# Rows of softmax maxima written into the query operand by one masked VectorE instruction instead of a copy and a transfer

## The chip, the cores and the metric

One core of a Trainium2 chip runs the whole program. The metric is device time in microseconds (us) of one execution, the median over repeated runs. Engines are named as in the profile: PE is TensorE, PEld its weight loads, DVE is VectorE, ACT is ScalarE, POOL is GpSimd, SP is SyncE, which only issues transfers here. All transfers of ACT's and SP's queues share 16 DMA engines.

## The reference, cut to what matters

Two decoder layers over 2048 tokens of width 1024. Layer 0 mixes tokens by multi-head latent attention (12 heads, 64 + 32 rotary key columns), layer 1 by forgetting attention (12 heads of 64, with a cumulative log forget gate added to the logits). Each layer also has 4 heads of cross-attention into 256 memory tokens. All are softmax attentions:

```python
s = einsum('bqhd,bkhd->bhqk', q_i, k) * scale          # + F[t] - F[s] in layer 1
s = where(key_pos <= q_pos, s, -inf)                   # not for memory heads
p = softmax(s, axis=-1)
out = einsum('bhqk,bkhd->bqhd', p, v)
```

Then the heads are gated by silu(gate), projected, normalised and added to the residual stream. The softmax needs, for each query, some number close to its maximal logit that is subtracted before the exponential.

## The kernel before, in words

Layer 0 runs `proj_a` (input projection), `up_a` (up-projection of the latents to q, k and v), `attention`, `out_proj`; layer 1 runs `proj_b`, `attention`, `out_proj`. Float32 operands are split into a high and a low part (`hi` L195, `lo` L214), so that products of rounded parts add up to nearly full precision (`mm3` L247 issues three products for one). Outside the attention the tile framework orders the instructions of every engine by its own estimate of times; inside `run_units` the order is the one in which the code is written (L1151, `manual_schedule`).

An attention is cut into units (`Unit`, L1470): one head and 512 queries, 4 units a causal head and 4 a memory head, 64 units a layer. A unit goes through these steps.

- `q_dma` (L1483): SP loads the queries into an operand of the unit (head dimensions on partitions, 512 queries in the free dimension). Operands are a ring of a few tiles.
- `max_closures` (L1517): for each 128 queries, score products (L1560, for memory heads L1537) of 512 keys at a time go to PSUM, and DVE reduces each to its maximum (L1526). `nm` (L1569) joins several chunks (L1571). The result is a tile `nm` of 128 queries by 4 columns, negated.
- `nm_row` (L1573): one product with the identity (L1576) turns the 128x4 tile into 4 rows of 128 in PSUM, DVE copies them to a small tile `nr` (L1578), and ACT's queue issues a transfer of 2 KB (L1579) that lays the four rows one after the other into a single partition of the query operand, `nmrow`, right behind the head dimensions (partition 64 or 96). The key operand has a row of ones there (`k_ones` L1034, in layer 1 the first of the rows `fr` that `forget` stores at L986), so that the logit product itself subtracts the maximum.
- the logits: `s_logits` (L1677) with two or three products a block (`passes`, L1686), keys on PSUM partitions and queries in the free dimension; ACT's exponential reads PSUM (L1628, in the early units L1668), ACT copies to f16 (L198), POOL or DVE takes the remainder (L220).
- the values: `pv_steps` (L1689, products at L1702), `finish` (L1706) with the division and, every second head, a store by SP.

In layer 1 the key operand holds 9 rows behind the 64 head dimensions: the ones and 8 forget rows. `attention` (L1061) builds in each query tile `qb` the matching rows `ind`, one for the two forget rows of the unit's block and zero elsewhere; the row of maxima is written over the first of them. The maxima themselves use a copy of the operand in which that row stays zero.

Some memory units run before the attention proper, from `att_start` (L1002) through `run_early` (L1236), among the last projection products: 8 in layer 0, 12 in layer 1 (`MEM_EARLY`, L50). There the query loads are issued two units ahead and the rows of maxima one unit ahead. The others stand in the attention's list behind certain units (`MEM_AFTER`, L52); `MEM_FIRST` (L51) would put some at its front and is 0.

`run_units` (L1269) walks through the logit steps of all units in order and puts between them the score products of later units, up to `AHEAD` = 5 units ahead, as many columns as the ratio of score to logit columns and a lead demand. The `nm_row` of a unit is put in after 1024 more score columns (`ROW_AFTER`, L1281), and at the latest before the unit's own logits (L1376). On each engine the instructions are then executed in that order: what stands behind a waiting instruction waits too.

Names in the profile: `bA`, `bR`, `bQ`, `bG`, `bS` are views of the large slots of the on-chip memory (queries, keys, probabilities and `nr` alike), `banks` is PSUM, `idr` the identity, `nm` and `mx` the maxima, `frd` the forget rows, `qbs`, `qs`, `qms`, `vsp`, `ws` tensors in device memory.

Of the kernel before, what the change touches and what calls it, by code (L numbers as in the profile page):

```python
# [39 lines left out]
MEMW = 256  # L40
MEMH = 4
VC = 2 * DH + 1
EPS = 1e-6
THETA = 10000.0
LEAD = {0: 5.0, 1: 5.0}
# [1 line left out]
AHEAD = 5  # L47
MORE_Q = 6
PV_AHEAD = 120
MEM_EARLY = {0: 8, 1: 12}  # L50
MEM_FIRST = {0: 0, 1: 0}  # L51
MEM_AFTER = {0: (2, 3), 1: (1, 3)}  # L52
POOL_SHARE = {"mla": 0.45, "fox": 0.75, "mem": 0.5}
RUNUP = 1.7
ROW_AFTER = 1024
VALUES_AFTER = 3 * 1024
LOGP = 8.0 * math.log(2.0)
NEG = -1.0e30
# [130 lines left out]
class Trunk:  # L189
# [64 lines left out]
    def constants(self, ctx):  # L254
        tc, nc = self.tc, self.nc
        cp = self.cp = ctx.enter_context(tc.tile_pool(name="consts", bufs=1))
        self.pool = ctx.enter_context(tc.tile_pool(name="slots", bufs=1))
        self.psum = ctx.enter_context(tc.tile_pool(name="banks", bufs=1, space=PSUM)).tile([P, 8 * G], F32, name="banks")
        self.sm = ctx.enter_context(tc.tile_pool(name="small", bufs=3))
        idf = cp.tile([P, P], F32, name="idf")  # L260
        nc.gpsimd.memset(idf, 0.0)
        nc.gpsimd.affine_select(out=idf, in_=idf, compare_op=ALU.not_equal, fill=1.0, base=0,
                                pattern=[[-1, P]], channel_multiplier=1)
        idr = cp.tile([P, P], F32R, name="idr")
        nc.vector.tensor_copy(idr, idf)
        idb = cp.tile([P, P], BF16, name="idb")
        nc.vector.tensor_copy(idb, idf)
        mkq = cp.tile([P, P], BF16, name="mkq")
        nc.gpsimd.memset(mkq, 0.0)
        nc.gpsimd.affine_select(out=mkq, in_=mkq, compare_op=ALU.is_ge, fill=NEG, base=0,  # L270
                                pattern=[[1, P]], channel_multiplier=-1)
        self.mqk = cp.tile([P, P], BF16, name="mqk")
        nc.gpsimd.memset(self.mqk, 0.0)
        nc.gpsimd.affine_select(out=self.mqk, in_=self.mqk, compare_op=ALU.is_ge, fill=NEG, base=0,
                                pattern=[[-1, P]], channel_multiplier=1)
        ones = cp.tile([P, P], F32, name="ones")
        nc.gpsimd.memset(ones, 1.0)
        self.vmax = [cp.tile([P, 1], F32, name=f"vmax{l}") for l in range(4)]
        self.vscale = [cp.tile([P, 2], F32, name=f"vsc{l}") for l in range(4)]
        for t in self.vmax:  # L280
            nc.vector.memset(t, 0.0)
        nc.scalar.activation(cp.tile([P, 1], F32, name="one"), ones[:, 0:1], AF.Sqrt)
        self.idf, self.idr, self.idb, self.mkq, self.ones = idf, idr, idb, mkq, ones
        dp = ctx.enter_context(tc.tile_pool(name="scratch", bufs=1, space=DRAM))
        self.cs = dp.tile([P, 5, 2, S], F32, name="cs")
        self.qs = [dp.tile([P, 2, S], F32, name=f"qs{c}") for c in range(6)]
        self.ks = [dp.tile([P, 2, S], F32, name=f"ks{c}") for c in range(6)]
        self.qrs = dp.tile([HEADS, 2, HR, 2, S], F32, name="qrs")
        self.krs = dp.tile([ROPE, 2, S], F32, name="krs")
        self.qbs = [dp.tile([P, 2, S], F32, name=f"qbs{c}") for c in range(6)]  # L290
        self.kbs = [dp.tile([P, 2, S], F32, name=f"kbs{c}") for c in range(6)]
        self.fr = dp.tile([HEADS, 1 + 2 * NG, S], F32R, name="frd")
        self.vs = [dp.tile([S, HEADS * DH], F32, name=f"vs{l}") for l in range(2)]
        self.vsp = dp.tile([HEADS, P, NT, VC + 1], F16, name="vsp")
        self.qms = [[dp.tile([P, 2, S], F32, name=f"qms{l}_{c}") for c in range(2)] for l in range(2)]
        self.gs = [dp.tile([S, D], F32, name=f"gs{l}") for l in range(2)]
        self.kms = [dp.tile([DH, 2, MEMH, NMEM], F32, name=f"kms{l}") for l in range(2)]
        self.vms = [dp.tile([NMEM, MEMW], F32, name=f"vms{l}") for l in range(2)]
        self.ys = [dp.tile([S, D], F32, name=f"ys{l}") for l in range(2)]
        self.ws = dp.tile([KC, 2, P, D], F32, name="ws")  # L300
        self.h1 = [dp.tile([P, D], F32, name=f"h1_{t}") for t in range(NT)]
        self.cos, self.sin = (cp.tile([P, NT, HR], F32, name=x) for x in ("cos", "sin"))
        self.gq = cp.tile([P, 5], F32, name="gq")
        self.ssq = cp.tile([P, 2, NT], F32, name="ssq")
        self.rtok = cp.tile([P, 2, NT], F32, name="rtok")
# [645 lines left out]
    def forget(self, tp, tb, fpp, fl):  # L951
# [31 lines left out]
        nc.vector.tensor_copy(one, self.ones[0:HEADS, 0:1].to_broadcast([HEADS, G]))  # L983
        for b in range(NG):
            sl = slice(b * G, (b + 1) * G)
            nc.gpsimd.dma_start(out=self.fr[:, 0, sl], in_=one)  # L986
            for g in range(NG):
                d = tb.tile([HEADS, G], F32, name="fd", tag="fd")
                nc.vector.tensor_scalar(d, F[:, sl], F[:, g * G:g * G + 1], -math.sqrt(DH), op0=ALU.subtract, op1=ALU.mult)
                dh = tb.tile([HEADS, G], F32R, name="fdh", tag="fdh")  # L990
                nc.vector.tensor_copy(dh, d)
                dl = tb.tile([HEADS, G], F32R, name="fdl", tag="fdl")
                self.lo("dve", dl, d, dh)
                nc.gpsimd.dma_start(out=self.fr[:, 1 + 2 * g, sl], in_=dh)
                nc.gpsimd.dma_start(out=self.fr[:, 2 + 2 * g, sl], in_=dl)

    def load_r(self, dst, src):

# [3 lines left out]
    def att_start(self, l):  # L1002
# [14 lines left out]
        ap["qq"] = Turn(*(Later(lambda b=b, k=k: b.tile([P, 2, G], F32R, name=f"qq{k}")) for k, b in enumerate(qqs)))  # L1017
        ap["ymp"], ap["sp"] = ymp, sp
        ap["ym"] = Turn(*(ymp.tile([P, 4, 2 * DH], F32, name=f"ym{k}") for k in range(4)))
        ap["nr"] = Turn(*(nrp.tile([4, P], F32R, name=f"nr{k}") for k in range(4)))  # L1020
        ap["vrm"] = Turn(vrp.tile([P, MEMH * NMEM // P, DH], F32, name="vrm"))
        ap["pm"], ap["ps"], ap["pv"] = self.banks(2, 3), self.banks(5, 6), self.banks(0)
        self.l, self.yt = l, {}
# [8 lines left out]

    def k_ones(self, j):
        k = self.k_t[j]  # L1034
        row = k[DH:DH + 1, 1] if j == "m" else k[QK:QK + 1, 0] if self.l == 0 else None
        if row is not None:
            for b in range(0, row.shape[-1], G):
                self.hi("pool", row[:, b:b + G], self.ones[0:1, 0:1].to_broadcast([1, G]))

    def v_ones(self, j):  # L1040
        self.nc.gpsimd.memset(self.v_t[j][:, :, 2 * DH:VC + 1], 1.0)
# [18 lines left out]

    def attention(self):  # L1061
        nc, l, ap, B = self.nc, self.l, self.ap, self.box
        nb = DH + 1 + 2 * NG
        v0, yb = self.v0, B("A6" if l == 0 else "R0")
        ap["y"] = Turn(*(yb.tile([P, 4, 2 * DH], F32, name=f"y{k}") for k in range(4)))
        self.kv_place("1", B("A3" if l == 0 else "A6", r=True), yb if l == 0 else B("Q"))
# [7 lines left out]
        if l:  # L1074
# [2 lines left out]
            qb = B("A3", r=True), B("A0", r=True)  # L1077
            self.qb_t = [qb[j // NG].tile([nb, 2, G], F32R, name=f"qb{j}") for j in range(2 * NG)]
            for g in range(NG):
                ind = v0.tile([1 + 2 * NG, G], F32, name="ind")  # L1080
                nc.gpsimd.memset(ind, 1.0)
                for lo_b, hi_b in ((-(1 + 2 * g), 0), (0, 2 + 2 * g)):
                    nc.gpsimd.affine_select(out=ind, in_=ind, compare_op=ALU.is_ge, fill=0.0, base=lo_b + hi_b,
                                            pattern=[[0, G]], channel_multiplier=1 if lo_b else -1)
                for j in (g, g + NG):
# [150 lines left out]
def run_early(mem, objs):  # L1236
# [11 lines left out]
    def ends(m):  # L1248
        while len(pend) > m:
            o, s, box, _ = pend.pop(0)  # L1250
            with K.tc.high_priority(offset=PV_AHEAD):
                o.pv_steps([(s, box)])
            o.finish()
    for u in objs[:2]:
        u.q_dma()
    rows(objs[0])
    for k, u in enumerate(objs):
        if k + 2 < len(objs):
            objs[k + 2].q_dma()
        if k + 1 < len(objs):  # L1260
            rows(objs[k + 1])
        for pre, f, _ in u.main_closures():
            pre()
            f(pend)
# [133 lines left out]
class Head:  # L1398
# [7 lines left out]
    def prep(self):  # L1406
# [29 lines left out]

        def k_const():
            if kind == "fox":
                K.load_r(kt[DH:DH + 1 + 2 * NG, 1], K.fr[h].bitcast(F32))

        def v_load(a, b):
            nc.sync.dma_start(out=vt[:, a:b], in_=K.vsp[h, :, a:b])
# [27 lines left out]
class Unit:  # L1470
# [12 lines left out]
    def q_dma(self):  # L1483
# [5 lines left out]
        if self.kind == "fox":  # L1489
            src = K.qbs[h // 2][r, :, sl]  # L1490
            qa = self.q.get()
            qb = K.qb_t[g + NG * (h % 2)]
            nb = DH + 1 + 2 * NG
            K.load_r(qb[0:DH], src)
            K.load_r(qa, src[:, 0].unsqueeze(0).to_broadcast([2, DH, G]))
            self.mx_ops = ((qb[:, 0], nb), (kb, nb))
            self.nmrow = qb[DH:DH + 1, 1]
            self.passes = [((ka, P), (qa, P)), ((kb, nb), (qb[:, 1], nb))]
            return
        qq = self.q.get()  # L1500
# [1 line left out]
        if self.kind == "mla":  # L1502
            K.load_r(qq[0:NOPE], K.qs[h // 2][r, :, sl])
            K.load_r(qq[NOPE:QK], K.qrs[h, :, :, :, sl])
            self.nmrow = qh[QK:QK + 1]
            self.passes = [((ka, QK + 1), (qh, QK + 1)), ((kb, QK), (qh, QK)), ((ka, QK), (ql, QK))]
            self.mx_ops = ((qh, QK), (ka, QK))
        else:
            src = K.qms[l][h // 2][r, :, sl]
            K.load_r(qq[0:DH], src)  # L1510
            K.load_r(qh[DH:P], src[:, 0])
            self.nmrow = ql[DH:DH + 1]
            self.passes = [((ka, P), (qh, P)), ((kb, DH + 1), (ql, DH + 1))]
            self.mx_ops = ((qh, DH), (kb, DH))


    def max_closures(self):  # L1517
# [2 lines left out]
        out = []  # L1520

        def start():
            self.nmv = K.sm.tile([P, 4], F32R, name="nm", tag="nm", bufs=AHEAD + 2)

        def reduce(to, ps, negate):
            nc.vector.tensor_reduce(out=to, in_=ps, axis=AX.X, op=ALU.max, negate=negate)  # L1526
# [45 lines left out]

    def nm_row(self):  # L1573
        K, nc = self.K, self.K.nc
        ps = K.ap["pm"].tile([4, P], F32, name="pn", tag="pm")
        nc.tensor.matmul(ps, lhsT=self.nmv, rhs=K.idr, start=True, stop=True)  # L1576
        nr = K.ap["nr"].next()
        nc.vector.tensor_copy(nr, ps)  # L1578
        nc.scalar.dma_start(out=self.nmrow.bitcast(F32), in_=nr.bitcast(F32))  # L1579
        self.has_row = True  # L1580


# [189 lines left out]
```

## Time and profile before

| | |
|---|---|
| median of 3 runs | 3008.41 us (3008.02 to 3008.82) |
| the profiled execution, its own time | 2990.69 us |
| its span, first to last instruction | 2989.0 us |
| mean granted clock of TensorE | 0.964 of full speed |
| busy: PE, DVE, ACT, POOL | 2844.8, 1518.0, 1321.7, 1232.2 us |
| bytes moved | 398.13 MB, mean 133 GB/s |

The profile is of one execution. Busy time is the sum of an engine's instructions; matmuls are pipelined and their ends modelled, so PE can look full a little early. The granted clock is the share of 2.4 GHz that the chip let TensorE have in a stretch; it has two levels, 1.2 and 2.4 GHz, so a mean between 0.5 and 1 is a mixture. A wait is put down to what came last before the waiting instruction started. `ACTq` and `SPq` are the instructions of these engines' queues that issue transfers.

### The profile page before, as it was taken

How to read it: one execution, taken by the hardware profiler on the slowest of the kernel's cores; microseconds unless marked ns; L12 is line 12 of the kernel's file. 1: busy time of each engine (PE TensorE's matmuls, PEld its weight loads, DVE VectorE, ACT ScalarE, POOL GpSimd, SP SyncE). 2: the span in 40 equal slices, each digit the busy share in tenths (PEclk: the TensorE clock that was granted, in tenths of full speed). 3: DMA queues.
4: the chain of work that ended last, by engine and by line, in shares of the span. 5: the costliest groups of instructions: out<-in, count | busy, mean ns of one | idle time of the engine just before them, and what ended most of it. 6: DMA issues, size and time to landing. Idle time of an engine off the chain costs nothing. (4 is left out here: it accounts for less than half of the span.)

```text
span 2989.0 us, 59098 instructions
## 1 busy us (share of the span) xinstructions
PE 2844.8 (95%) x24401; PEld 2397.8 (80%) x24401; DVE 1518.0 (51%) x2954; ACT 1321.7 (44%) x1873; POOL 1232.2 (41%) x819
## 2 busy tenths in 40 slices
PE   7999999879999999999999999999979999989998
PEld 6789998657878888878889988998757777867787
DVE  6422215556776777644453364200357757757344
ACT  5321123336777777842240010111237877868321
POOL 2110124335677777752100023100227767768521
PEclk9999999978999999999999999999969999989999
DMA  5332347761334233265343138723434434344453
GB/s 187 127 131 90 126 163 254 256 186 37 96 81 105 69 95 83 55 211 195 124 152 108 61 108 284 249 76 100 140 88 110 121 94 125 102 145 126 172 179 116
DMA packets 261502, 398.13 MB, mean 133 GB/s; under 512 B 25028, under 2 KB 141268, under 8 KB 261124
## 3 DMA queue, kind: packets, MB, share of 16 engines
q1 hardware_dynamic: 180040, 254.92, 30.0%
q10 hardware_dynamic: 80040, 138.54, 12.6%
q8 instruction: 192, 3.15, 0.4%
q0 software_dynamic: 1152, 0.89, 0.2%
q14 instruction: 78, 0.64, 0.1%
HBM read 237.83 MB, written 156.17 MB: 132 GB/s over the span
## 5 line engine op out<-in xcount | busy, mean ns | idle before, releaser
L220 POOL TENSOR_TENSOR bA<-bA,bA 128x1024 f16<-128x1024 f32 (+5 forms) x277 | 503.3, 1829 | 372.6 <-ACT bA L198 250.2
L1526 DVE TENSOR_REDUCE mx<-banks 128x1 f32<-128x512 f32 (+2 forms) x864 | 511.4, 617 | 254.4 <-PE banks L1560 251.7
L251 PE MATMUL banks<-bR,bA 128*128 128x256 f32 (+3 forms) x4437 | 553.0, 287 | 0.6 <-DVE bQ L496 0.6
L251 PEld LDWEIGHTS banks<-bR,bA 128*128 128x128 f32 x4437 | 544.4, 190 | 5.5 <-DVE bQ L496 0.8
L251 PE MATMUL banks<-bA,bR 128*128 128x512 f32 (+2 forms) x2208 | 513.6, 389 | 6.2 <-ACT bS L809 4.1
L1686 PE MATMUL banks<-bA,bA 96*128 96x512 f32 (+13 forms) x1808 | 495.2, 385 | 24.6 <-DMA bA<-bA 11.3
L251 PEld LDWEIGHTS banks<-bA,bR 128*128 128x128 f32 x2208 | 403.1, 191 | 92.3 <-ACT bS L809 4.5
L1628 ACT ACTIVATE bA<-banks 128x1024 f32<-128x1024 f32 (+1 forms) x409 | 364.3, 891 | 253.5 <-PE banks L1686 143.8
L1686 PEld LDWEIGHTS banks<-bA,bA 96*128 96x128 f32 (+3 forms) x1808 | 332.2, 197 | 90.0 <-issue 23.4
L198 ACT ACTIVATE bA<-bA 128x1024 f16<-128x1024 f32 (+5 forms) x400 | 335.7, 846 | 92.5 <-DMA qrs<-bA 18.9
L1560 PE MATMUL banks<-bA,bA 73*128 73x512 f32 (+5 forms) x864 | 334.7, 427 | 5.6 <-DMA bA<-qbs 3.2
L205 POOL TENSOR_SCALAR bR<-bR 128x1024 fp32r<-128x1024 f32 (+3 forms) x50 | 60.3, 1208 | 407.7 <-PE banks L251 371.5
L1702 PEld LDWEIGHTS <-bA 128*128 128x128 f16 x5918 | 203.0, 100 | 31.0 <-issue 15.1
L1207 PE MATMUL banks<-bA,bA 128*128 128x512 f32 x960 | 227.2, 392 | 0.0
L1686 PE MATMUL banks<-bR,bA 128*128 128x512 f32 (+6 forms) x624 | 209.5, 402 | 14.3 <-DMA bR<-bA 10.4
L1207 PEld LDWEIGHTS banks<-bA,bA 128*128 128x128 f32 x960 | 179.1, 188 | 36.2
L220 POOL TENSOR_TENSOR bR<-bR,bR 128x1024 f16<-128x1024 f32 (+2 forms) x75 | 160.9, 2145 | 81.5 <-ACT bR L198 42.6
L1178 POOL TENSOR_TENSOR bA<-bA 128x512 f32<-128x512 f32 x64 | 97.5, 1545 | 214.7 <-DMA bA<-gs 204.0
L1560 PEld LDWEIGHTS banks<-bA,bA 73*128 73x128 f32 (+1 forms) x864 | 168.0, 202 | 21.3 <-DVE mx L1526 4.4
L220 POOL TENSOR_TENSOR bR<-bA,bR 128x1024 f16<-128x1024 f32 (+2 forms) x74 | 149.9, 2027 | 80.9 <-ACT bR L198 29.5
L220 DVE TENSOR_TENSOR bR<-bR,bR 128x1024 fp32r<-128x1024 f32 (+5 forms) x66 | 81.8, 1243 | 187.0 <-POOL bR L205 167.6
L494 ACT ACTIVATE bG<-banks 128x256 f32<-128x256 f32 x128 | 48.9, 383 | 287.8 <-PE banks L251 221.1
(224 smaller groups left out, 3667.8 us busy)
## 6 DMA issues: line engine op xcount, KB each, us to landing
bA<-qbs SPq DMA_DIRECT2D x65, 256.0 KB
bA<-in_x_dram SPq DMA_DIRECT2D x32, 512.0 KB
gs<-bG ACTq DMA_DIRECT2D x128, 128.0 KB
bA<-gs SPq DMA_DIRECT2D x32, 512.0 KB
bA<-ys SPq DMA_DIRECT2D x32, 512.0 KB
bA<-h SPq DMA_DIRECT2D x28, 512.0 KB
ks<-bA ACTq DMA_DIRECT2D x24, 512.0 KB
qs<-bA ACTq DMA_DIRECT2D x24, 512.0 KB
```

Source lines behind the costliest of these rows:

```text
L198: nc.scalar.activation(out, in_, AF.Copy, scale=scale)
L205: nc.gpsimd.tensor_scalar(out, in_, scale, 0.0, op0=ALU.mult, op1=ALU.add)
L220: e.tensor_tensor(out=out, in0=in_, in1=hi, op=ALU.subtract)
L251: nc.tensor.matmul(out, lhsT=a, rhs=b, start=start and i == 0, stop=stop and i == n - 1)
L494: nc.scalar.activation(st[:, 0:2 * P], ps[:, 0:2 * P], AF.Silu)
L1178: nc.gpsimd.tensor_tensor(out=gt[:, hs], in0=gt[:, hs], in1=yt[:, hs], op=ALU.mult)
L1207: nc.tensor.matmul(ps[:, ns], lhsT=a, rhs=b[:, ns], start=c == 0 and j == 0, stop=c == KC - 1 and j == 2)
L1526: nc.vector.tensor_reduce(out=to, in_=ps, axis=AX.X, op=ALU.max, negate=negate)
L1560: nc.tensor.matmul(ps, lhsT=q[0:qr, t * P:(t + 1) * P], rhs=k[0:kr, x:x + w], start=not diag, stop=True, skip_group_check=diag)
L1628: nc.scalar.activation(pf[:, 0:w], ps[:, 0:w], AF.Exp, scale=self.scale, bias=LOGP)
L1686: nc.tensor.matmul(ps[:, o:o + bw], lhsT=k[0:kr, (self.k0 + kt) * P:(self.k0 + kt + 1) * P], rhs=q[0:qr, q0:q0 + bw], start=i == 0 and not ...
L1702: nc.tensor.matmul(self.pv[:, t, 0:n], lhsT=p[:, o:o + P], rhs=v[:, kv, a:a + n], start=self.first, stop=False, skip_group_check=True)
```

## The change

`nm_row` keeps its one product but gives it a wider weight operand. All tiles of maxima now are 4-column slices of one tile `nmw` whose first 128 columns are zero, 7 slices in turn (`NMS` = `AHEAD` + 2). The weights are the `at + 4` columns that end with the unit's slice (`at` is 64, or 96 for the latent heads), so the four rows come out on PSUM partitions `at` to `at + 3`. There one DVE instruction multiplies them, repeated four times along the free dimension by a zero stride, with a mask `spread` (4x4 identity, each element repeated 128 times by a zero stride) and writes 4 rows of 512 into the query operand: row r holds the maxima of queries 128 r to 128 r + 127 and zeros elsewhere. The copy to `nr`, the tiles `nr` and the transfer on ACT's queue are gone. The keys get four rows of ones instead of one (`NR` = 4), the forget rows move back by three and the operands of layer 1 have 76 partitions instead of 73 (`FB` = 12); `forget` stores the row of ones four times.

Three more things change: `MEM_EARLY` goes from 8 and 12 units to 6 and 8, `MEM_FIRST` from 0 to 4 in both layers, and `run_early` loads queries three units ahead and makes rows two units ahead.

```diff
@@ constants of the module @@
+NR = 4
+FB = NR + 2 * NG
...
-MEM_EARLY = {0: 8, 1: 12}
-MEM_FIRST = {0: 0, 1: 0}
+MEM_EARLY = {0: 6, 1: 8}
+MEM_FIRST = {0: 4, 1: 4}
...
+NMS = AHEAD + 2
@@ constants() @@
+        self.nmw = cp.tile([P, P + 4 * NMS], F32R, name="nmw")
+        self.spread = cp.tile([P, NR], F32, name="spread")
+        nc.gpsimd.memset(self.spread, 1.0)
+        for base in (DH, QK):
+            b = slice(base, base + 32)
+            for sign in (1, -1):
+                nc.gpsimd.affine_select(out=self.spread[b], in_=self.spread[b], compare_op=ALU.is_ge, fill=0.0, base=0,
+                                        pattern=[[-sign, NR]], channel_multiplier=sign)
...
+        nc.vector.tensor_scalar(self.nmw[:, 0:P], ones, 0.0, None, op0=ALU.mult)
+        nc.vector.tensor_scalar(self.nmw[:, P:P + 4 * NMS], ones[:, 0:4 * NMS], 0.0, None, op0=ALU.mult)
+        self.nmk = 0
...
-        self.fr = dp.tile([HEADS, 1 + 2 * NG, S], F32R, name="frd")
+        self.fr = dp.tile([HEADS, FB, S], F32R, name="frd")
@@ forget() @@
-            nc.gpsimd.dma_start(out=self.fr[:, 0, sl], in_=one)
+            for r in range(NR):
+                nc.gpsimd.dma_start(out=self.fr[:, r, sl], in_=one)
@@ att_start() @@
-        ap["nr"] = Turn(*(nrp.tile([4, P], F32R, name=f"nr{k}") for k in range(4)))
@@ k_ones() @@
-        row = k[DH:DH + 1, 1] if j == "m" else k[QK:QK + 1, 0] if self.l == 0 else None
+        row = k[DH:DH + NR, 1] if j == "m" else k[QK:QK + NR, 0] if self.l == 0 else None
         if row is not None:
             for b in range(0, row.shape[-1], G):
-                self.hi("pool", row[:, b:b + G], self.ones[0:1, 0:1].to_broadcast([1, G]))
+                at = DH if j == "m" else QK
+                self.hi("pool", row[:, b:b + G], self.ones[at:at + NR, 0:1].to_broadcast([NR, G]))
@@ run_early() @@
+    for u in objs[:3]:
+        u.q_dma()
     for u in objs[:2]:
-        u.q_dma()
-    rows(objs[0])
+        rows(u)
     for k, u in enumerate(objs):
+        if k + 3 < len(objs):
+            objs[k + 3].q_dma()
         if k + 2 < len(objs):
-            objs[k + 2].q_dma()
-        if k + 1 < len(objs):
-            rows(objs[k + 1])
+            rows(objs[k + 2])
@@ Unit.q_dma(), the memory heads (the other kinds alike) @@
-            self.nmrow = ql[DH:DH + 1]
-            self.passes = [((ka, P), (qh, P)), ((kb, DH + 1), (ql, DH + 1))]
+            self.nmrow, self.at = ql[DH:DH + NR], DH
+            self.passes = [((ka, P), (qh, P)), ((kb, DH + NR), (ql, DH + NR))]
@@ Unit.max_closures() @@
-            self.nmv = K.sm.tile([P, 4], F32R, name="nm", tag="nm", bufs=AHEAD + 2)
+            self.nms = 4 * (K.nmk % NMS)
+            K.nmk += 1
+            self.nmv = K.nmw[:, P + self.nms:P + self.nms + 4]
@@ Unit.nm_row() @@
-        ps = K.ap["pm"].tile([4, P], F32, name="pn", tag="pm")
-        nc.tensor.matmul(ps, lhsT=self.nmv, rhs=K.idr, start=True, stop=True)
-        nr = K.ap["nr"].next()
-        nc.vector.tensor_copy(nr, ps)
-        nc.scalar.dma_start(out=self.nmrow.bitcast(F32), in_=nr.bitcast(F32))
+        at, end = self.at, self.at + NR
+        ps = K.ap["pm"].tile([end, P], F32, name="pn", tag="pm")
+        a = P - at + self.nms
+        nc.tensor.matmul(ps, lhsT=K.nmw[:, a:a + end], rhs=K.idr, start=True, stop=True)
+        nc.vector.tensor_tensor(out=self.nmrow.rearrange("r (t q) -> r t q", t=NR),
+                                in0=ps[at:end, None, :].to_broadcast([NR, NR, P]), in1=K.spread[at:end, :, None].to_broadcast([NR, NR, P]), op=ALU.mult)
```

## Rows read from the trace of the kernel before

**Rows 1.** The page, first part: busy time, share of the span, instructions.

```profile
PE 2844.8 (95%) x24401; PEld 2397.8 (80%) x24401; DVE 1518.0 (51%) x2954; ACT 1321.7 (44%) x1873; POOL 1232.2 (41%) x819
```

**Rows 2.** Waits of PE: waiting line, releaser: us in total, times, longest.

```profile
PE banks L1686 <- DMA bA<-bR: 17.3, 4, 5.7
PE banks L1648 <- ACT bA L1628: 16.8, 4, 9.1
PE banks L1686 <- DMA bA<-bA: 13.1, 11, 5.8
PE banks L1686 <- DMA bR<-bA: 10.4, 5, 2.9
...
PE banks L1686 <- ACT bA L1628: 8.5, 7, 2.7
...
PE banks L1560 <- DMA bA<-qbs: 3.2, 3, 1.3
```

**Rows 3.** Stretches: length, busy PE, PEld, DVE, ACT, POOL (instructions), clock, DMA, GB/s.

```profile
615.00:705.00 90.00, 68.37 (x453) 50.09 (x454) 46.74 (x101) 34.82 (x46) 31.70 (x22) 0.66 0.42 122
705.00:1275.00 570.00, 569.20 (x6947) 462.23 (x6944) 402.81 (x730) 443.40 (x538) 419.90 (x218) 1.00 0.33 83
2160.00:2265.00 105.00, 81.88 (x658) 56.98 (x657) 63.30 (x130) 45.12 (x54) 40.45 (x29) 0.72 0.38 98
2265.00:2775.00 510.00, 478.27 (x6215) 380.58 (x6214) 345.01 (x641) 392.95 (x443) 380.87 (x182) 0.95 0.44 124
```

**Rows 4.** Source view of L1579: who waited for it (us, times).

```profile
  PE banks L1686: 40.9, 20
```

**Rows 5.** Timeline, 637 to 643: start us, us, engine, line, instruction [idle before <- releaser].

```profile
637.04 0.28 DVE L1578 CAST bR<-banks 4x128 fp32r<-4x128 f32 x1
...
637.36 0.62 ACTq L1579 DMA_DIRECT2D bA<-bR  x1
...
642.75 0.79 PE L1686 MATMUL banks<-bA,bR 65*128 65x512 f32 x1 [5.74 <-DMA bA<-bR]
```

**Rows 6.** Timeline, 2616 to 2632.

```profile
2616.20 5.58 SPq L1442 DMA_DIRECT2D bQ<-vsp  x2
...
2619.04 0.27 DVE L1578 CAST bA<-banks 4x128 fp32r<-4x128 f32 x1
...
2621.83 6.68 SPq L999 DMA_DIRECT2D bA<-qbs  x4
...
2630.53 0.58 ACTq L1579 DMA_DIRECT2D bA<-bA  x1
2631.21 1.02 ACT L1628 ACTIVATE bA<-banks 128x1024 f32<-128x1024 f32 x1 [12.93 <-DMA bQ<-vsp]
```

**Rows 7.** Groups by line and form: busy us, mean ns of one | idle before.

```profile
L251 PEld LDWEIGHTS banks<-bA,bA 128*128 128x128 f32 x468 | 85.4, 190 | 31.5 <-DVE bA L824 6.5 <-ACT bS L809 5.5 <-DVE bA L817 3.2
...
L1578 DVE CAST bA<-banks 4x128 fp32r<-4x128 f32 x64 | 17.4, 272 | 20.2 <-PE banks L1576 20.2
...
L824 DVE TENSOR_TENSOR bA<-banks,bR 128x512 f32<-128x512 f32 x24 | 16.3, 684 | 4.1 <-PE banks L251 3.9
...
L1576 PEld LDWEIGHTS banks<-idr,nm 128*4 128x4 f32 x128 | 11.4, 89 | 6.9 <-DVE nm L1526 1.7 <-DVE nm L1571 1.7 <-DVE bA L1715 0.2
```

**Rows 8.** Timeline, 2122 to 2127: products of one early memory unit.

```profile
2123.24 0.50 PE L1537 MATMUL banks<-bA,bR 64*128 64x256 f32 x2
...
2125.40 0.90 PE L1702 MATMUL banks<-bA,bA 128*128 128x65 f16 x24
```

**Rows 9.** Source view of L986: ns min/median/max; what ended its idle time.

```profile
L986 POOL DMA_DIRECT2D frd<-bA x4: 518/521/726, 1566.1 to 1567.8; - x4
...
  DVE bA L983: 117.7, 1
```

**Rows 10.** Timeline, 4 to 4.5 us.

```profile
4.27 1.06 ACT L323 ACTIVATE bA<-bA 128x1024 fp32r<-128x1024 f32 x1 [1.96 <-DMA bA<-in_x_dram]
```

**Rows 11.** Waits of ACT between 705 and 1275 us.

```profile
ACT bA L1628 <- PE banks L1686: 60.7, 73, 1.9
```

More of the change, by code (lines that the diff above doesn't have):

```diff
@@ L993, in forget @@
                 self.lo("dve", dl, d, dh)
-                nc.gpsimd.dma_start(out=self.fr[:, 1 + 2 * g, sl], in_=dh)
-                nc.gpsimd.dma_start(out=self.fr[:, 2 + 2 * g, sl], in_=dl)
+                nc.gpsimd.dma_start(out=self.fr[:, NR + 2 * g, sl], in_=dh)
+                nc.gpsimd.dma_start(out=self.fr[:, NR + 1 + 2 * g, sl], in_=dl)
     def load_r(self, dst, src):
@@ L1062, in attention @@
         nc, l, ap, B = self.nc, self.l, self.ap, self.box
-        nb = DH + 1 + 2 * NG
+        nb = DH + FB
         v0, yb = self.v0, B("A6" if l == 0 else "R0")
@@ L1079, in attention @@
             for g in range(NG):
-                ind = v0.tile([1 + 2 * NG, G], F32, name="ind")
+                ind = v0.tile([FB, G], F32, name="ind")
                 nc.gpsimd.memset(ind, 1.0)
-                for lo_b, hi_b in ((-(1 + 2 * g), 0), (0, 2 + 2 * g)):
+                for lo_b, hi_b in ((-(NR + 2 * g), 0), (0, NR + 1 + 2 * g)):
                     nc.gpsimd.affine_select(out=ind, in_=ind, compare_op=ALU.is_ge, fill=0.0, base=lo_b + hi_b,
@@ L1438, in k_const @@
             if kind == "fox":
-                K.load_r(kt[DH:DH + 1 + 2 * NG, 1], K.fr[h].bitcast(F32))
+                K.load_r(kt[DH:DH + FB, 1], K.fr[h].bitcast(F32))
         def v_load(a, b):
@@ L1492, in q_dma @@
             qb = K.qb_t[g + NG * (h % 2)]
-            nb = DH + 1 + 2 * NG
+            nb = DH + FB
             K.load_r(qb[0:DH], src)
@@ L1496, in q_dma @@
             self.mx_ops = ((qb[:, 0], nb), (kb, nb))
-            self.nmrow = qb[DH:DH + 1, 1]
+            self.nmrow, self.at = qb[DH:DH + NR, 1], DH
             self.passes = [((ka, P), (qa, P)), ((kb, nb), (qb[:, 1], nb))]
@@ L1504, in q_dma @@
             K.load_r(qq[NOPE:QK], K.qrs[h, :, :, :, sl])
-            self.nmrow = qh[QK:QK + 1]
-            self.passes = [((ka, QK + 1), (qh, QK + 1)), ((kb, QK), (qh, QK)), ((ka, QK), (ql, QK))]
+            self.nmrow, self.at = qh[QK:QK + NR], QK
+            self.passes = [((ka, QK + NR), (qh, QK + NR)), ((kb, QK), (qh, QK)), ((ka, QK), (ql, QK))]
             self.mx_ops = ((qh, QK), (ka, QK))
```

## The prediction

> **What bounds the kernel now.** The page's first part comes first: TensorE (PE) is busy 95% of the span, no other engine over 51%, so the kernel is paced by PE and a change pays where PE stands still or runs slowly [rows 1]. PE's waits say on whom: 17.3 + 13.1 + 10.4 = 40.8 us of logit products (L1686) wait for a DMA whose source and target are the kernel's own slots, and 16.8 + 8.5 us for ACT's exponentials (L1628) [rows 2]. The source view of L1579, the 2 KB transfer that puts the row of maxima into the query operand, gives it as that DMA: PE waited 40.9 us for it in 20 places [rows 4].
>
> The stretches say where. I count a stretch's loss as its length less busy time times granted clock (work at 2.4 GHz; 0.5 would be 1.2 GHz throughout) [rows 3]:
> - **A**, 615 to 705 us, end of the first layer's up-projection and start of its attention: 90 - 68.37 x 0.66 = 44.9 us lost.
> - 705 to 1275, that attention in full flow: 570 - 569.2 = 0.8 us.
> - **B**, 2160 to 2265, start of the second layer's attention: 105 - 81.88 x 0.72 = 46.0 us.
> - **C**, 2265 to 2775, its full flow: 510 - 478.27 x 0.95 = 55.6 us.
> In A and B the clock is the larger part: PE pauses, the grant falls, and what follows runs at near half rate.
>
> One row in A shows the wait. DVE copies it from PSUM at 637.04 (0.28 us), ACT issues the transfer at 637.36 (0.62), and the logits that need it start at 642.75, after 5.74 us of PE idling [rows 5]. Issue and landing took 5.4 us of it.
>
> C differs. There a row was copied at 2619.04, but ACT issued its transfer only at 2630.53; SP's queue stood in load issues all that time (two took 5.58 us, the next four 6.68), and ACT's exponential, queued behind that issue, came 12.93 us late and held PE for 9.1 us [rows 2, 6]. The profile names a load of values as ACT's releaser. Thus ACT is held by a small transfer that waits for large ones.
>
> **The change, part by part.**
> - **Transfers removed.** 128 issues of about 0.6 us [rows 5] leave ACT's queue, and the landing leaves the chain. In A the waits were 17.3 us [rows 2]. If nothing but they went, each replaced by about 1 us of DVE latency, A would gain 17.3 - 4 = 13. If all loss went, 45. A floor lies between: DVE was busy 46.74 us in A, and with 9 rows at +0.41 us 50 us [rows 3], so A cannot fall much below 50 while filling its pipeline. I take the middle of 77 (90 - 13) and 50, that is 64: **gain 26**. In B the waits were about 20 of the remaining 23.5 us (rows of the second layer) [rows 2]; alone 20 - 9 = 11, so 94; DVE floor 63.30 + 15 x 0.41 = 69 [rows 3]; the middle is 81: **gain 24**. Behind the row, exponentials and the next maxima are late next.
> - **C.** The ACT waits are 16.8 + 8.5 us and the row's own about 3 [rows 2]: 28 us. The bounds are 0 (the loads themselves were late, PE then waits for them) and 55.6. I take the 28 plus about a third of the remaining 28 of slow clock after them: **gain 36**. The big loads stay in SP's queue, so query loads (3.2 us of PE's waits now [rows 2]) are what comes late next.
> - **The VectorE instruction.** The copy of 4x128 took 272 ns [rows 7]; the new one writes 4x512 from PSUM with a mask. The nearest row is a two-operand instruction on 512 elements a partition from PSUM, 684 ns [rows 7]: +0.41 us, 128 times, 53 us of DVE. DVE is busy 402.81 of 570 us in the first full flow and 345 of 510 in the second [rows 3], which hides it there. Where it waits for its product, reductions of the next unit stand behind it and PE waits for their PSUM banks; the copy stood in the same place. Fewer partitions or the zero-stride operand could make it as short as the copy (0), and nothing gives less. In the 10 rows before A and B, which lie among projections, logits now follow DVE closely: 10 x 0.41 = **4 us lost**.
> - **The product.** Its weights are 68 or 100 columns, not 4. Loading 4 took 89 ns and 128 took 190 [rows 7], so 0.81 ns a column: +52 ns for 80 rows, +78 ns for 48, together 7.9 us of weight load, part beside running products. Bounds 0 and 8: **4 us lost**. The Trainium skill (TensorE: Matmul & The Clock Gate, LDWEIGHTS) makes a weight load's time proportional to columns, P/1.2 ns; its slope would give 80 x 53 + 48 x 80 ns = 8.1 us, an estimate from that page and a rule that speaks against the change. The rows agree in slope, not in proportion: 4 columns take 89 ns, not 3. By the page alone, nothing hidden, the sum would be 4 us higher.
> - **Moved units.** Two memory units in the first layer and four in the second leave the early part; four in each layer now open the attention. Each issues two SP loads, four score products (0.50 us a pair), one row, four logit products of twice that width, 24 value products (0.90 us) [rows 8]: about 3.5 us of PE, with two exponential passes on ACT and a remainder now wholly on POOL. Their work only moves: 21 us of PE leave A, B or the projections before and come back in the flow. I price this at 0; cover is PE's spare time in A and B, and if the flow paid it all while A and B kept their length it would cost 21. In the early part loads run three units ahead and rows two, which covers DVE's latency; SP's store of a finished pair stands behind them, but nothing waits on it there.
> - **At nothing.** The keys' four rows of ones: the weight loads have the same columns, POOL's instructions the same length per partition. Twelve more POOL stores of the ones at 0.52 us: the four now stand after 117.7 us of POOL idling [rows 9]; uncovered, 6 us. SP's 12 loads of forget rows grow by a third. The constants (memset, four selects, two small DVE products) run before the first data, when ACT starts at 4.27 us [rows 10]; uncovered, 2 us.
>
> Sum: 26 + 24 + 36 - 4 - 4 = 78 us off the profiled execution (2990.7, span 2989.0), which itself lies 17.7 us under the median of 3008.4. I carry the difference over to the median: **2930 us**.
>
> **Rivals.**
> 1. *DVE takes the row's place at the starts.* For: in B it is already busy 63 of 105 us. Against: in A it idles half the time [rows 3]. A and B then give only 13 + 11: 3008 - (24 + 36 - 8) = 2956. Chance 0.20.
> 2. *C's wait is the loads'.* If the operands loaded behind SP's queue are what is truly late, PE waits for them and C gives nothing: 3008 - (50 - 8) = 2966. For: SP stood in issues for 5 us; against: PE waits only 3.2 us for queries now. Chance 0.14.
> 3. *All loss goes.* Without gaps the clock stays at 2.4 GHz through A, B and C: 3008 - (45 + 46 + 56 - 8) = 2869. Against: DVE's floor. Chance 0.10.
> 4. *The first flow speeds up too.* PE looks full there, but weight loads fill 462 of 570 us, 81% [rows 3]. If ACT's issue time were on the path, 51 rows x 0.6 = 31 us more: 2899. Against: ACT waits for PE's logits there, 60.7 us in one group alone [rows 11]. Chance 0.05. The Trainium skill (Perfetto Trace Analysis, Identifying the Most-Contended Engine) holds matmul busy time to be a poor measure and the weight-load share the better one, and would allow this; rows 11 do not support it.
> 5. *Slower: DVE sets the pace.* DVE is in order, so 0.41 us in front of each unit's reductions delays the PSUM banks that PE needs. If every row paid it, 53 + 8 = 61 us; the starts would give nothing (the row waits for DVE instead of the transfer) and C only ACT's 25: 3008 + 36 = 3044. It decides from (25 - 8)/0.41, some 40 of the 128 rows, on the path. Against: DVE is busy at most 71% in the flows [rows 3]. Chance 0.08.
> 6. *Nothing changes:* the chain keeps its length, because the logits wait for something beside the row. 3008, chance 0.06.
>
> **How the numbers follow.** The forecast keeps 0.37. Rivals 1 to 4 and it are faster: 0.86; rival 6 is the same, 0.06; rival 5 slower, 0.08. A measurement here tells 0.2% (6 us) from no change. The range runs from rival 3's 2868 to 2978, past rival 2; it leaves out rivals 5 and 6 and a little more.
>
> **What would show it.** Right: no L1579, no PE wait on a DMA between own slots; the new DVE instruction at 0.6 to 0.75 us; A and B some 25 us shorter with a granted clock above 0.8; in C no exponential held more than 3 us behind an issue, clock near 1. Wrong: PE waiting for the new instruction by name at many rows, for query loads in C, or DVE over 90% busy at the starts; and a first flow longer than 570 us by more than its moved units.

## The result, and the profile after

The median went from 3008.22 us (four runs of before) to 2928.43 (four runs, 2922.26 to 2935.74): ratio 0.9742, 95% interval 0.9713 to 0.9771. The profiled execution took 2922.26 us (span 2920.2), 68.4 less than the one of before, and the mean granted clock rose from 0.964 to 0.975.

Part 1 of the page and PE's waits in the whole span, answering to [rows 1] and [rows 2]; L1705 are the logit products, L1578 and L1555 score products, L1596 the row's product, L1597 the new VectorE instruction, L1647 the exponential:

```profile
PE 2822.9 (97%) x24401; PEld 2394.5 (82%) x24401; DVE 1556.6 (53%) x2950; ACT 1324.8 (45%) x1867; POOL 1249.0 (43%) x836
```

```profile
PE banks L1555 <- DMA bA<-qms: 5.9, 3, 3.5
PE banks L1596 <- DVE nmw L1544: 5.6, 5, 1.8
...
PE banks L1705 <- ACT bR L1687: 4.9, 1, 4.9
PE banks L1578 <- DMA bA<-qbs: 4.6, 2, 2.7
...
PE banks L1578 <- DMA bA<-qrs: 2.4, 1, 2.4
PE banks L1578 <- DVE bA L1597: 2.0, 7, 0.3
...
PE banks L1596 <- DVE bA L1597: 1.1, 1, 1.1
...
PE banks L1705 <- ACT bA L1647: 0.8, 1, 0.8
...
PE banks L1705 <- DVE bR L1597: 0.3, 1, 0.3
```

The 40.8 us in which logit products waited for a row have become 0.3, and 25.3 us of waits for L1628's exponentials have become 0.8. In their place stand loads of queries (12.9 us), one early exponential (4.9) and something new, 5.6 us in which the row's product waits for a maximum in `nmw`. The new instruction itself is waited for 3.4 us in all.

The four stretches, moved to where the same parts of the program now lie, answer to [rows 3]:

```profile
600.00:690.00 90.00, 74.16 (x538) 54.69 (x538) 61.10 (x117) 37.54 (x50) 37.66 (x27) 0.73 0.56 156
690.00:1265.00 575.00, 571.25 (x6913) 467.81 (x6910) 408.03 (x727) 443.67 (x538) 418.50 (x218) 0.99 0.32 78
2145.00:2205.00 60.00, 56.61 (x373) 40.43 (x373) 47.46 (x87) 25.28 (x30) 26.17 (x20) 0.63 0.49 130
2205.00:2705.00 500.00, 487.36 (x6521) 393.06 (x6519) 382.58 (x682) 414.40 (x462) 399.06 (x190) 0.99 0.48 131
```

Lost (length less busy time times clock): A 35.9 us (44.9 before), the first flow 9.5 (0.8), B 24.3 (46.0), C 17.5 (55.6). So C gives 38, B 22, A 9, and the first flow takes 8.7 back: 60 us of the 68.8 by which the spans differ. The clock is printed with two digits, so over 500 us and more such a loss is good to some 3 us only.

The forms of the new operations, answering to [rows 7] (weight load of 68 and of 100 columns, the VectorE instruction):

```profile
L1597 DVE TENSOR_TENSOR bA<-banks,spread 4x512 fp32r<-4x512 f32 x108 | 74.7, 692 | 25.7 <-PE banks L1596 23.7
...
L1596 PEld LDWEIGHTS banks<-idr,nmw 128*68 128x68 f32 x80 | 12.2, 152 | 9.3 <-DVE nmw L1544 4.5 <-DVE bA L1597 1.4 <-issue 0.9
...
L1596 PEld LDWEIGHTS banks<-idr,nmw 128*100 128x100 f32 x48 | 8.2, 171 | 5.2 <-DVE nmw L1544 3.3 <-DVE mx L1544 0.4
```

To follow where time goes in each run I use three marks: the start of the last value product of the first attention, of the last projection product of `proj_b`, and of the last value product of the second attention. "Second attention" below is the third less the second. One profile stands behind each mark; executions of one kernel differ by 3 to 22 us, so differences of a few us say nothing. A ratio compares a run with executions of before taken along with it, whose medians were 2999 to 3008 us; so ratios compare two runs better than their medians do.

| run | median us | ratio to before, 95% | first attention ends | second attention |
|---|---|---|---|---|
| before | 3008.2 | 1 | 1289.9 | 635.9 |
| **the change** | 2928.4 | 0.9742 (0.9713 to 0.9771) | 1282.6 | 575.8 |
| e1 row's new way alone | 2942.4 | 0.9803 (0.9779 to 0.9827) | 1281.8 | 598.0 |
| e2 new places alone | 2962.5 | 0.9879 (0.9849 to 0.9908) | 1277.3 | 629.3 |
| e3 transfer on POOL's queue | 2984.3 | 0.9942 (0.9927 to 0.9958) | 1294.6 | 626.9 |
| e4 new instruction twice | 2961.9 | 0.9874 (0.9844 to 0.9904) | 1298.2 | 599.8 |
| e10 copy added | 2930.3 | 0.9769 (0.9754 to 0.9783) | 1285.0 | 585.4 |
| e5 two strips | 2921.9 | 0.9733 (0.9711 to 0.9756) | 1286.5 | 571.9 |
| e6 strips, old places in layer 0 | 2913.7 | 0.9711 (0.9684 to 0.9737) | 1286.6 | 575.8 |
| e7 strips, fresh query tiles | 2918.9 | 0.9730 (0.9712 to 0.9749) | 1281.5 | 571.6 |
| e8 strips, 4 early units a layer | 2905.4 | 0.9689 (0.9667 to 0.9710) | 1268.9 | 577.7 |
| e12 strips, 4 and 8 early | 2910.7 | 0.9696 (0.9671 to 0.9721) | 1270.8 | 575.0 |
| e9_two strips, 2 and 8 early | 2930.6 | 0.9771 (0.9756 to 0.9786) | 1286.4 | 577.5 |
| e9_none strips, none early | 2946.6 | 0.9823 (0.9808 to 0.9837) | 1302.4 | 599.8 |

### The profile page after: what moved, and what is told of

Read it like the earlier page. It is cut to its first block, busy times and chain, and to the rows that moved or that the text cites. A ratio compares the mean times of both kernels' runs of the same rounds, so it can differ in the third digit from the quotient of the medians.

```text
span 2920.2 us, 58773 instructions
## 1 busy us (share of the span) xinstructions
PE 2822.9 (97%) x24401; PEld 2394.5 (82%) x24401; DVE 1556.6 (53%) x2950; ACT 1324.8 (45%) x1867; POOL 1249.0 (43%) x836
## 5 line engine op out<-in xcount | busy, mean ns | idle before, releaser
L1705 PE MATMUL banks<-bA,bA 96*128 96x512 f32 (+13 forms) x1820 | 484.1, 377 | 0.9 <-ACT bA L1647 0.8
L1647 ACT ACTIVATE bA<-banks 128x1024 f32<-128x1024 f32 (+1 forms) x414 | 370.9, 896 | 201.2 <-PE banks L1705 177.3
L1705 PEld LDWEIGHTS banks<-bA,bA 96*128 96x128 f32 (+3 forms) x1820 | 327.7, 193 | 43.4 <-ACT bA L1647 1.7
L1578 PE MATMUL banks<-bA,bA 76*128 76x512 f32 (+5 forms) x868 | 335.4, 424 | 10.0 <-DMA bA<-qbs 4.6
L1705 PE MATMUL banks<-bR,bA 128*128 128x512 f32 (+6 forms) x620 | 202.3, 393 | 0.6 <-DVE bR L1597 0.3
L223 POOL TENSOR_TENSOR bR<-bR,bR 128x1024 f16<-128x1024 f32 (+2 forms) x74 | 160.0, 2162 | 89.6 <-ACT bR L201 48.0
L1578 PEld LDWEIGHTS banks<-bA,bA 76*128 76x128 f32 (+1 forms) x868 | 167.4, 200 | 24.2 <-issue 9.9
```

The source lines that it names most:

```text
L223: e.tensor_tensor(out=out, in0=in_, in1=hi, op=ALU.subtract)
L1578: nc.tensor.matmul(ps, lhsT=q[0:qr, t * P:(t + 1) * P], rhs=k[0:kr, x:x + w], start=not diag, stop=True, skip_group_check=diag)
L1647: nc.scalar.activation(pf[:, 0:w], ps[:, 0:w], AF.Exp, scale=self.scale, bias=LOGP)
L1705: nc.tensor.matmul(ps[:, o:o + bw], lhsT=k[0:kr, (self.k0 + kt) * P:(self.k0 + kt + 1) * P], rhs=q[0:qr, q0:q0 + bw], start=i == 0 and not ...
```

## The experiments

### The two halves of the change, each alone

e1 is the changed kernel with the old places and order, e2 the kernel before with the new ones (`run_early` accordingly):

```diff
-MEM_EARLY = {0: 6, 1: 8}
-MEM_FIRST = {0: 4, 1: 4}
+MEM_EARLY = {0: 8, 1: 12}
+MEM_FIRST = {0: 0, 1: 0}
```

> The new way of the row alone: units stand and run ahead as in the kernel before (8 and 12 early units, none first, loads two and rows one unit ahead). Theory T (the transfer's removal pays; it held ACT's in-order queue in the second layer's flow): most of the 80 us come, 2935 to 2960; from the last product of proj_b to the end of the second attention 575 to 600 us (kernel before 634, changed kernel 574); no exponential held by a DMA; first layer within 10 us of the changed kernel's. Rival P (the new places of the memory units pay, the row's way hardly): 2985 to 3008 and over 620 us between the two marks.

> The new places and the longer run-ahead alone, with copy and transfer of the kernel before. Theory T: 2985 to 3015, over 615 us from the last product of proj_b to the end of the second attention, PE still waiting some 15 to 40 us in all for rows that come by DMA and for exponentials that ACT held behind a row's issue. Rival P: 2930 to 2955 and under 590 us between the marks.

Measured: the row's way alone gives 1.97% of the 2.58%, the new places alone 1.21%. Theory T's range for e1 holds. For e2 both theories were wrong about the total: 2962.5 lies between theirs; its second attention, 629.3, is as T had it. By medians the halves together would give more than the change, so they pay in part for the same time. In the second attention, by the marks of single profiles (e2's is the slowest of its four executions), it is the other way round: 37.9 us from the row's way, 6.6 from the places, 60.1 from both.

ACT's waits in the second flow, first of e2 (2215 to 2760 us), then of e1 (2245 to 2728):

```profile
ACT bA L1629 <- PE banks L1687: 45.5, 59, 3.2
ACT bA L1629 <- DMA bA<-qbs: 19.5, 4, 6.7
...
ACT bA L1629 <- DMA bQ<-vsp: 14.0, 2, 12.9
```

```profile
ACT bA L1646 <- PE banks L1704: 66.2, 101, 4.4
ACT bA L1646 <- POOL bA L223: 5.3, 4, 2.6
```

The changed kernel has, from 2205 to 2705 us:

```profile
ACT bA L1647 <- PE banks L1705: 62.1, 107, 3.7
```

With the transfer, ACT idles for loads that it never reads, wherever the units stand; without it, it waits for no DMA there, mostly for its logits. C is nearly the row's alone: e1 loses 483 - 471.65 x 0.98 = 20.8 us in that stretch. The start is not, as start and flow show, first of e1, then of e2:

```profile
2150.00:2245.00 95.00, 90.13 (x637) 65.10 (x638) 67.52 (x123) 41.59 (x50) 38.41 (x27) 0.59 0.39 102
2245.00:2728.00 483.00, 471.65 (x6243) 381.06 (x6242) 364.33 (x648) 397.61 (x446) 383.39 (x183) 0.98 0.48 131
```

```profile
2145.00:2215.00 70.00, 58.69 (x381) 40.82 (x380) 45.62 (x96) 27.10 (x32) 27.92 (x22) 0.63 0.46 124
2215.00:2760.00 545.00, 510.75 (x6545) 405.75 (x6545) 359.67 (x678) 412.51 (x463) 399.79 (x191) 0.94 0.43 119
```

e1 has PE busy 90 of 95 us, and yet loses 41.8 us there: the waits are gone, the clock stays at 0.59. e2 loses 33.0 in a start of 70 us, and C's loss (64.9) is no smaller than before. B's full gain needs both, no waits and a shorter start. The new places are three edits (fewer early units, four units first, a longer run-ahead); which of them shortens this start was not tried.

The first layer is different. By the marks the new places alone bring the end of its attention 12.6 us forward, the row's new way alone 8.1, and both together 7.3. Its start, first of e1, then of e2:

```profile
615.00:705.00 90.00, 83.25 (x591) 61.30 (x590) 61.60 (x120) 42.37 (x56) 37.46 (x24) 0.70 0.47 127
```

```profile
600.00:690.00 90.00, 79.31 (x552) 57.81 (x551) 58.38 (x124) 40.21 (x54) 41.45 (x30) 0.73 0.61 172
```

They lose 31.7 and 32.1 us, against 44.9 before and 35.9 after the change. So each half alone gives A some 13 us, and both together give no more.

### The transfer on another queue

```diff
-        nc.scalar.dma_start(out=self.nmrow.bitcast(F32), in_=nr.bitcast(F32))
+        nc.gpsimd.dma_start(out=self.nmrow.bitcast(F32), in_=nr.bitcast(F32))
```

> Kernel before, but the row's transfer is issued by POOL's queue in place of ACT's. Theory T (what costs in the second flow is ACT standing behind an issue that waits): ACT's exponentials are no longer held by a DMA (14 + 12 + 16 us of such idling in the kernel before), the waits of PE for the row's landing at the starts stay (some 20 us and the clock behind them), 2965 to 2990. Rival Q (the row's landing itself is what is late, whoever issues it): the waits of logits on the row grow, 3000 or more. Rival R (POOL takes ACT's place: remainders stand behind the held issue): no DMA among ACT's releasers, but values wait for POOL's remainders over 30 us, 3000 or more.

2984.3 us, in T's range. PE's waits in the second flow, before (2265 to 2775) and e3 (2265 to 2770):

```profile
PE banks L1648 <- ACT bA L1628: 16.8, 4, 9.1
PE banks L1686 <- ACT bA L1628: 7.8, 6, 2.7
PE banks L1686 <- DMA bA<-bA: 2.8, 6, 0.9
```

```profile
PE banks L1686 <- DMA bA<-bA: 13.8, 9, 2.3
PE banks L1560 <- DMA bA<-qbs: 4.2, 3, 1.9
```

The 24.6 us that PE waited for ACT are gone entirely, but 11 us of waits for the landing row come up behind them (rival Q in part). The transfer and the data that it needs are those of before, and no logit product here waits for it over 2.3 us; so the long holds came with its place in ACT's queue. The stretch loses 505 - 484.67 x 0.96 = 39.7 us, against 55.6 before and 17.5 after the change. So of C's 38 us some 16 are ACT held by the issue, and the other 22 come only when the landing goes too. This split is rough: PE stands still 20.3 us in e3's stretch and 31.7 in that of before, so 11 of the 16 are idle time, and the rest hangs on two-digit means of the clock. The whole kernel gains 0.58%.

### What the VectorE instruction costs

e4 issues it twice; e10 puts a 4x128 copy of the same PSUM tile behind it.

```diff
+        for _ in range(2):
+            nc.vector.tensor_tensor(out=self.nmrow...
...
+        nc.vector.tensor_copy(K.dummy[at:end], ps[at:end])
```

> Changed kernel with the new VectorE instruction issued twice (0.69 us more of DVE per row, 88 us in all). Theory T (DVE has room wherever rows are made): 2928 to 2940, DVE's busy time up by 88 us. Rival D (DVE's order is on the path, so the instruction itself cost the change a good part of what it brought): each repetition shows, 2970 to 3016.

> Changed kernel with an extra copy of 4x128 behind the new instruction, on the same PSUM tile (0.27 us a row, 35 us of DVE in all), which is two thirds of the 0.41 us that the new instruction is longer than the old copy. Theory E (there is an edge: the bank comes free in time up to about 0.7 us of DVE, and what goes beyond costs): little, 2928 to 2934, waits of score products for that instruction 2 to 4 us. Rival D (each us of DVE in that place costs 0.38 us of time, as the doubled instruction did on the mean): 2940 to 2945.

e4 is 33.4 us above the change by medians (40 by ratios): T is wrong, DVE's room is small; D's range, from 2970 on, is missed too. PE's waits of e4 (its L1598 is the new instruction, L1577 and L1578 scores):

```profile
PE banks L1578 <- DVE bA L1598: 11.5, 17, 1.0
...
PE banks L1577 <- DVE bA L1598: 4.0, 5, 0.9
PE banks L1555 <- DVE bA L1598: 3.8, 2, 2.4
```

With five smaller rows these are 22.9 us, against 3.4 in the change. The row's tile lies in the same ring of PSUM banks as the scores, and doubled it no longer frees its bank in time. The named waits grow by 19.5 us; where the rest of the 33 goes was not found. e10 stands 1.9 us above the change by medians, 8 by ratios, with overlapping intervals; waits on the added copy are 5.3 us, where E had 2 to 4. So 35 us of extra DVE cost 2 to 8, and 88 us cost 33 to 40: the price rises with length, as E has it, but a price of D's size is excluded only by medians. That the instruction at its own length stands just before an edge fits these numbers and is not shown.

### The shared window

The weights of one row reach over the lower slots of `nmw`, so a unit in a high slot also reads slot 0, which the next unit may already be filling. At 749.77 us of the changed kernel:

```profile
749.77 0.43 PE L1596 MATMUL banks<-idr,nmw 128*100 128x128 f32 x1 [1.76 <-DVE nmw L1544]
```

Three such waits, 3.6 us, lie in the first flow, and behind this one the clock falls for a while with PE busy throughout, worth another 3.3 us:

```profile
750.00:780.00 30.00, 30.00 (x350) 24.78 (x350) 18.80 (x35) 20.06 (x23) 18.47 (x9) 0.89 0.31 75
```

e5 has two tiles `nmw` of four slots each (`NMS` = 4), used in turn:

```diff
+        self.nmw = [cp.tile([P, P + 4 * NMS], F32R, name=f"nmw{k}") for k in range(2)]
...
+            self.nms = 4 * (K.nmk // 2 % NMS)
+            self.nmt = K.nmw[K.nmk % 2]
```

> Changed kernel with two strips of maxima used in turn, so that no row's product covers the slot that the next unit has begun to write. Theory S (PE's waits at the new product for the first maxima of the following unit, 5.6 us in 5 places, come from the slots shared in one window): these waits fall under 1.5 us, PE's grant no longer dips behind them, 2918 to 2928. Rival (the product waits for its own unit's last maxima): the waits stay and the time is that of the changed kernel, 2928.

The waits of the row's product for a following unit's maximum are gone from the list, and the first flow is full again, a loss of 0.4 us where the change had 9.5:

```profile
690.00:1265.00 575.00, 574.62 (x6999) 470.72 (x6999) 414.65 (x742) 447.66 (x541) 421.43 (x220) 1.00 0.33 81
```

S is right about the waits. In the total, 2921.9, it cannot be told from the change. e1 has the shared window too and loses only 2.3 us in its first flow, 1.1 of them in such a wait, at a clock of 1.00; so the waits are the window's, and the size of the loss depends on whether the clock falls behind them.

### The start of the first attention

e6 gives the first layer its old places (`MEM_EARLY` 8, `MEM_FIRST` 0), e7 lets the first memory units take query tiles that no early unit holds (`early = [later(...)] + few`), e8 to e9_none vary the early units; all with two strips.

```diff
-MEM_EARLY = {0: 6, 1: 8}
+MEM_EARLY = {0: 4, 1: 4}
```

> Two strips, and in the first layer alone the old places (8 early memory units, none first). Theory L (in the first layer the memory units put first wait for their queries' loads and bring nothing): the first attention ends within 3 us of the two-strip kernel's or up to 6 earlier, no PE wait on the load of memory queries, total 2915 to 2930. Rival M (they cover the start there as in the second layer): it ends 10 to 20 us later, 2935 to 2945.

> Two strips, and the memory units at the attention's front take the fresh query tiles (A7; R2 and R3 in the second layer) ahead of those that the early units still hold. Theory L (the start of the first attention waits for loads that stand behind held tiles): PE's waits on loads of memory queries, 5.9 us, go, the grant rises sooner, first attention 8 to 15 us shorter, total 2905 to 2920. Rival K (the clock's low stretch there is not made by these waits): 2920 to 2930, the stretch from 600 to 690 us granted 0.75 or less as now.

> Two strips, four early memory units a layer in place of 6 and 8, four first as in the changed kernel. Theory B (in the early part PE runs at half clock though busy, so each unit taken out of it is worth the difference between half and full clock, some 3 us a unit): second attention 4 to 12 us shorter from the last product of proj_b on, total 2905 to 2920. Rival N (the early units fill idle time that PE has anyway; fewer of them leave it idle): the projections' end shows the idle time, 2930 or more.

> Two strips, two early memory units in the first layer and eight in the second, four first. Theory H: first attention's end between 1262 and 1272 us, second layer as in the two-strip kernel, total 2898 to 2910. Rival F: first attention's end 1275 us or later, total 2912 or more.

> Two strips, no early memory unit in either layer, four first. Theory H (the start costs what it costs because PE there runs at half clock while it fills its pipeline, whatever units stand there; early units only lengthen that stretch): first attention's end as early as with four early units or earlier, 1262 to 1270 us in the profile, total 2895 to 2908. Rival F (the first units' maxima and loads are what has to be covered; without early units PE idles at the projections' ends): PE idle between 600 and 680 us over 25 us, total 2915 to 2945.

> Two strips, four early units in the first layer, eight in the second, four first. Theory Z (the whole gain of four early units a layer is the first layer's, where the first attention ended at 1268.9 in place of 1286.5; in the second layer eight and four are alike): 2902 to 2909, first attention's end 1266 to 1274. Rival Y (the second layer's share is real: 6.5 us of shorter projections count): 2910 to 2917. Rival X (the four-unit result was a matter of how the clock fell in those executions and not of the order): 2918 to 2926, end at 1280 or later.

e6: no wait for memory queries, and the first attention ends where it does in e5, as L had it; the total, 2913.7, is 1 us below L's range. So that wait is not what costs. e7: its total, 2918.9, is in L's range and 1 us below K's, but L is wrong about the waits; PE waits for the same loads, now 10.4 us with one of 7.9. The granted clock from 600 to 690 is 0.72, as K had it, and the interval of the total is nearly e5's.

e8: 2905.4 us, the best here, and its interval lies below that of the change. The total is as theory B had it, but B is wrong about its source: the second attention is not shorter. The projections before it are 6.5 us shorter, it is 5.8 longer. The gain over e5 is the first layer's, whose attention ends 17.6 us earlier. Here are e5 and e8 at that start:

```profile
600.00:690.00 90.00, 73.28 (x490) 54.50 (x488) 62.17 (x115) 34.81 (x49) 35.96 (x27) 0.77 0.59 173
```

```profile
600.00:660.00 60.00, 44.71 (x253) 32.95 (x254) 38.49 (x77) 21.21 (x30) 23.31 (x19) 0.69 0.53 152
660.00:1250.00 590.00, 589.53 (x7157) 482.14 (x7154) 424.84 (x765) 457.94 (x553) 432.00 (x224) 1.00 0.35 84
```

e5 loses 33.6 us there and reaches the flow at about 690, e8 29.2 and is in the flow at 660. But not all of the 17.6 us is the early units'. The first 3200 products are the same in both kernels, and e5 is behind long before the attention, as the first 500 us of e5 and then of e8 show:

```profile
0.00:500.00 500.00, 467.12 (x2973) 425.65 (x2974) 180.01 (x406) 142.81 (x286) 92.77 (x126) 0.97 0.44 146
```

```profile
0.00:500.00 500.00, 468.41 (x3013) 426.86 (x3014) 185.15 (x415) 146.73 (x293) 96.65 (x130) 0.99 0.46 151
```

Product number 3200 starts at 553.4 us in e5, at 543.6 in e8, at 545.7 in e12 and at 546.1 in the change. From there to the end of the first attention e5 takes 733.1 us, e8 725.3, e12 725.1 and the change 736.5. So four early units in place of six are worth some 8 us, and the other 10 arose while PE did the same work in both, which points to scatter between executions.

e9_two and e9_none: F both times. With two early units one score product waits 8.1 us for latent queries, with none one waits 17.0, so the units do cover loads (PE idles 20.9 us from 600 to 680, less than F had, and the total, 2946.6, is 2 us above F's range). By the end of the first attention four is the best of 0, 2, 4 and 6. e12 repeats the first layer's gain (1270.8, as Z had it); its total of 2910.7 is in Y's range by 0.7 us, and its interval holds e8's median, so whether the second layer adds anything stays open.

## Why the prediction was right, and where not

The time, 2928.4 against 2930, and the sign were right. The sum against the profiled execution was 78 us and the profile shows 68.4; that the medians differ by 79.8 is the scatter of executions. The sum was too high by 17 in A and by 9 in the first flow, so that the median came out within 2 us of the forecast is luck. "In A and B the clock is the larger part" was misread: by the rows of before PE's idle time is 21.6 of 44.9 us in A and 23.1 of 46.0 in B, so clock and idle time share the loss about equally.

- **C, forecast 36, was 38**, and for the reason given: no exponential is behind an issue, PE waits for ACT's exponentials 0.8 us instead of 25.3, clock 0.99. e1 shows that the row's way alone does nearly all of it, e3 that ACT's hold is 16 of it. The step took the waits as the sum's core and a third of the clock's part; the landing's share, which e3 brings up, was not priced on its own.
- **B, forecast 24, was 22**, but not with "a granted clock above 0.8": it is 0.63. The start became shorter, not faster, and most of that needs the new places, which I had priced at 0: without them (e1) the start still loses 41.8 us. Size right, mechanism half right.
- **A, forecast 26, was 9.** The step that failed is "I take the middle of 77 and 50". The row's 17.3 us of waits went, and 5.9 + 2.4 us for query loads and 4.9 for an early exponential came. I had named exponentials as late next and not charged them; query loads I had named for C. The clock is 0.50 in both slices from 620 to 660, where before it was 0.50 and 0.82. My lower case, 13, was nearer, and it is what the row's way gives alone (e1). The moved units, priced at 0, give A as much alone (e2); with both, the two gains do not add. Why they do not was not settled.
- **The first flow, forecast 0, lost 8.7** by the count above, some 7 by its parts: 3.6 us of waits and 3.3 of lower clock. It is the shared window, which the prediction did not see; e5, without it, has neither.
- **The VectorE instruction**, 0.69 us as forecast. The 4 us, 3.4 by named waits, fit; "hides it there" in the flows is true at this length only, as e4 shows.
- **The product's weights**: 152 and 171 ns on the mean, 141 and 167 by my slope from [rows 7]. The means mix the two levels of the clock: outside the stretches at the lower one the medians are 140 and 164 ns, within them 188 and 242 (the last of 3 loads). It is 9.0 us more weight load in all, forecast 7.9. How much of it is on the path was not tried. The Trainium skill (TensorE: Matmul & The Clock Gate, LDWEIGHTS) makes the time proportional to the columns; 171 against 152 ns for 100 against 68 columns is not: its slope without a fixed part doesn't hold here.
- **Rivals.** DVE in the row's place (1): not at this length. Loads as C's true wait (2): no, 4.6 us for queries in the change. All loss gone (3): no, the starts keep their clock. First flow faster (4): no; e5 does 6999 products in its 575 us, about as many a us as the 6947 in 570 us of before. Slower by DVE (5): no, though twice the instruction takes nearly half the gain.

## What to carry to other kernels

A small transfer issued from a compute engine's queue costs its latency and can hold the engine's next instructions behind large loads, here an exponential for 12.93 us. Look for that engine idling for a DMA whose data it never reads, and before replacing the transfer move its issue to another queue to price the two parts apart. A start with a low clock isn't cured by removing its waits alone: vary how much work stands in it. When slices of one tile are read through a window, see which other slices it covers.

## What was not expected of the hardware

The clock stayed at its lower level with PE nearly always busy. The changed kernel from 2145 us:

```profile
2145.00:2160.00 15.00, 13.25 (x85) 8.40 (x84) 11.57 (x19) 5.12 (x8) 6.59 (x8) 0.75 0.40 121
2160.00:2175.00 15.00, 13.66 (x79) 10.13 (x79) 13.71 (x23) 4.19 (x6) 5.39 (x5) 0.50 0.52 138
2175.00:2190.00 15.00, 15.00 (x77) 10.64 (x77) 10.35 (x20) 7.41 (x8) 6.40 (x3) 0.50 0.40 109
```

The only pause over 1 us between 2148 and 2162 is one of 1.14 us at 2152.32, and from 2160 to 2190 the grant is 0.50, 1.2 GHz, with PE busy 28.7 of 30 us. e1 has the same for longer, 0.50 from 2165 to 2210 with 43.8 of 45 us busy. Busy time at the lower level counts longer instructions, so it hides the loss. Here are the same forms of logit product (L1705, half of them 128x512, half 68x512; ns shortest, median, longest), at the lower level and in the first flow:

```profile
L1705 PE MATMUL banks<-bA x8: 628/628/735, 2165.1 to 2174.1; 128*128 128x512 f32 x4, 68*128 68x512 f32 x4
```

```profile
L1705 PE MATMUL banks<-bA,bR x8: 390/395/396, 813.9 to 837.6; 128*128 128x512 f32 x4, 68*128 68x512 f32 x4
```

What brings the grant back up wasn't settled; in each of these kernels it is up once the attention's own flow runs.
